# The last tiles of an entry: one product's weight sums made earlier, one operand's sums put behind the last tile

## The chip, the cores and the metric

The kernel runs on one core of a Trainium2 chip. Its time is the device time of one execution in microseconds (us); the median of three runs is 1895.14 us (1893.95 to 1895.23). A profiled execution gives the trace from which all rows below are taken. The engines are TensorE (PE, with its weight loads as PEld), VectorE (DVE), ScalarE (ACT), GpSimd (POOL) and the queue of SyncE (SP), which issues most DMAs. Each works through its own instructions in order, and they wait for each other by semaphores.

## The reference

A decoder block on 1024 tokens of width 1024, in float32:

```python
h = h + 0.5 * swiglu(rms_norm(h, ffn1_norm), w1, w3, w2)          # D_FF = 2816
u = rms_norm(h, mix_norm);  proj = u @ w_in                       # q, k, v, p, gates
y_attn = dilated_mixture_attention(q, k, v) @ w_branch_attn
y_pool = multiscale_pool(p, pool_w, pool_scale) @ w_branch_pool
h = h + (sigmoid(gA) * y_attn + sigmoid(gB) * y_pool) @ w_out
h = h + 0.5 * swiglu(rms_norm(h, ffn2_norm), w1, w3, w2)
return rms_norm(h, final_norm)
```

Three stages concern us: the two up-projections of the FFNs (`x @ w1`, `x @ w3`) and the mixer's input projection (`u @ w_in`). Each begins with the normalised rows of h, which have to be transposed before TensorE can contract over features.

## The kernel before

**Seven products.** The large matrix products are cut into 2 x 2 blocks and computed with seven block products instead of eight (the Strassen-Winograd form). One half of the split is by tokens (512 and 512), the other by features. Of the left matrix x there are four blocks b11, b21 (tokens 0 to 511) and b12, b22 (tokens 512 to 1023) and four sums:

t1 = b12 - b11, t2 = b22 - t1, t3 = t2 - b11 = b22 - b12, t4 = t2 - b21.

In the code: `first_less` makes t1 (line 467), `second` t2 (471), `third` t3 (474, into the bank that held b12), `fourth` t4 (478). The products are numbered m = 1 to 7: m=1 uses b11, m=2 b21, m=6 t2, m=7 t3, m=5 t1, m=4 t4, m=3 b22. On the weights' side there are sums as well: s1 for m=5, s2 = s1 - a11 for m=6, s3 for m=7, s4 for m=3 (`Quad.summed`, lines 370 to 383); m=1, 2 and 4 take blocks of weights as they were loaded.

**High and low parts.** For accuracy each operand is split into a part rounded to the form `float32r` (high) and the rest (low), and each block product is three groups of four matmuls (line 332): high x high, weights' high x operand's low, weights' low x operand's high. ACT makes the high part by a copy (line 320 for weights, 411 and 433 for x), and DVE or POOL makes the low part by a subtraction (line 323 for weights; 416 and 436 for x). What is subtracted from a PSUM bank is always DVE's here.

**The entry.** At the head of each of the three stages stands an entry (`Entry.run`). The first 512 tokens are already transposed, and b11 and b21 are known. The second 512 tokens come in four tiles t = 4 to 7 of 128. Meanwhile PE has the products m=1 and m=2 of the first few column pairs to do, which need b11 and b21 only. Per tile, in this order: a product; four transposes for b22 (line 409) and four for b12 (line 485), into one PSUM bank each; the outputs of products; the four sums of x with their parts; a second product. The next tile's rows are scaled by the norm (line 282) in between. After the last tile come m=6, 7, 5, 4, 3, for which t2, t3, t1, t4 and b22 of all four tiles must be there. The entry is run for the first FFN (around 40 to 60 us of the span), for the mixer (around 657 to 678) and for the second FFN (around 1252 to 1276). The whole stretch is in an order written out by hand: each engine gets its instructions as the code names them.

Names in it: `operand(i)` splits the weights of the entry's i-th product (their low part on POOL), `product(i)` issues its matmuls, `out(i)` takes its bank to SBUF. `Rows` are transposes with their high part, `Parts` the high part (`higher`, ACT) and low part (`lower`, DVE unless POOL is named) of a sum. `more(0, 1)` makes s1 of the first product after the entry (DVE, line 370), `more(0, 2)` makes s2 (POOL, line 374), `more(0)` splits the weights of m=6 and `more(1)` those of m=7 (making s3 first, DVE, line 378). The low part of weights outside the entry goes to DVE for each third split and to POOL otherwise: m=6's low part is POOL's in the first FFN and the mixer and DVE's in the second FFN; m=5's is DVE's in the first FFN and POOL's in the other two.

PSUM has four banks under the tag "acc" (transposes, t2, products m=6, 7, 4) and four under "mm" (m=1, 2, 5, 3). Half tiles under the tag "s" (four of them) hold the sums of weights.

Of the kernel before, what the change touches and what calls it, by code (L numbers as in the profile page):

```python
# [137 lines left out]
def tile_block(  # L138
# [29 lines left out]
    ve, ac, gp, pe = nc.vector, nc.scalar, nc.gpsimd, nc.tensor  # L168

    def sbuf(name, side="left", bufs=1):  # L170
        return tc.tile_pool(name=name, bufs=bufs, side=side, reuse_waits="tile")
# [7 lines left out]
    def bank(tag, name):  # L179
        return psum.tile([P, HALF], F32, tag=tag, name=name)  # L180
# [18 lines left out]
    h = []  # L199
# [98 lines left out]
    LOWS, HIGHS = slice(0, HALF), slice(HALF, S)  # L298

    def sums_of_x(pool, name, order, **kw):  # L300
        return {
            s: tuple(pool.tile([P, 4, HALF], F32R, name=f"x{part}_{s}_{name}", **kw) for part in ("hi", "lo"))
            for s in order
        }
# [31 lines left out]
    class Quad:  # L336
# [49 lines left out]
        def run(self, m, back=True):  # L386
            if m not in self.w:
                self.operand(m)
            w, n = self.w.pop(m), self.n
            x = {1: "b11", 2: "b21", 3: "b22", 4: "t4", 5: "t1", 6: "t2", 7: "t3"}[m]  # L390
            key = {1: "x", 2: "x", 5: "v", 3: "v"}.get(m, m)
            first = key not in self.bank
            if first:
                self.bank[key] = bank("mm" if key in ("x", "v") else "acc", f"u_{self.sv.name}{n}{m}")
            self.sv.product(self.bank[key], w, x, start=first)
            if m == 3 and back:
                raws.back(2)
            return self.bank[key]
# [39 lines left out]
    class Entry:  # L438
# [18 lines left out]
        def run(self, high, after, first=0):  # L457


            X = self.sv.X  # L460

            def scaled_rows(t):
                return high(t, 1)

            def first_less(p12, t):
                t1 = h[t][:, LOWS]
                ve.tensor_tensor(t1, p12, self.low[t - 4][:, LOWS], op=OP.subtract)
                return t1

            def second(s, t1, t2):  # L470
                ve.tensor_tensor(t2, s.flat, t1, op=OP.subtract)

            def third(t2, p, t):
                ve.tensor_tensor(p, t2, self.low[t - 4][:, LOWS], op=OP.subtract)

            def fourth(t2, t):
                t4 = h[t][:, HIGHS]
                ve.tensor_tensor(t4, t2, self.low[t - 4][:, HIGHS], op=OP.subtract)
                return t4

            def turned(y, t):
                p12 = bank("acc", f"x_b12_{t}")
                for j in range(4):
                    c = slice(j * P, (j + 1) * P)
                    pe.transpose(p12[:, c], y[:, c], ident)
                return p12

            def turned_rows(y, t, tag="acc"):
                return Rows(X, "b22", y[:, HIGHS], t, tag)

            y = scaled_rows(4)
            self.operand(first + 2)
            r4 = None
            for t in range(4, NT - 1):
                i = first + 2 * (t - 4)
                k = i + 1
                self.product(i)
                high(t + 1, 0)
                s = turned_rows(y, t)
                p12 = turned(y, t)  # L500
                self.out(i)
                if r4 is not None:
                    r4.higher()
                    r4.lower(gp)
                t1 = first_less(p12, t)
                t2 = bank("acc", f"x_t2_{t}")
                s.lower()
                second(s, t1, t2)
                self.product(k)
                y = scaled_rows(t + 1)  # L510
                r2 = Parts(X, "t2", t2, t)
                r1 = Parts(X, "t1", t1, t)
                third(t2, p12, t)
                r1.lower(gp)
                self.operand(k + 2)
                r2.lower()
                self.out(k)
                r3 = Parts(X, "t3", p12, t)
                r3.lower()
                r4 = Parts(X, "t4", fourth(t2, t), t, False)  # L520
                after(t)
                self.operand(i + 4)
                if t > 4:
                    self.more(0, 1)

            t = NT - 1
            i, k = i + 2, k + 2
            self.product(i)
            p12 = turned(y, t)
            s = turned_rows(y, t, "mm")  # L530
            r4.higher()
            r4.lower(gp)
            t1 = first_less(p12, t)
            t2 = bank("acc", f"x_t2_{t}")
            second(s, t1, t2)
            self.more(0, 2)
            r2 = Parts(X, "t2", t2, t)
            third(t2, p12, t)
            self.more(0)
            self.out(i)  # L540
            r2.lower()
            r3 = Parts(X, "t3", p12, t)
            r3.lower()
            self.product(k)
            r1 = Parts(X, "t1", t1, t)
            r4 = Parts(X, "t4", fourth(t2, t), t, False)
            self.more(1)
            r1.lower()
            r4.higher()
            self.out(k)  # L550
            s.lower()
            r4.lower()
            after(t)


# [364 lines left out]
    X = sums_of_x(scope.enter_context(sbuf("x1")), "f1", SUMS)  # L920
# [1100 lines left out]
    with tc.manual_schedule():  # L2021
# [8 lines left out]
        for q in range(N // 2):  # L2030
# [20 lines left out]
            u, i = divmod(q, NT // 2)  # L2051
# [450 lines left out]
```

## Time and profile before

| what | value |
|---|---|
| median of three runs | 1895.14 us |
| profiled execution | 1895.29 us |
| its span | 1893.5 us |
| PE busy | 1875.3 us (99%) |
| DVE busy | 1346.6 us (71%) |
| ACT busy | 774.1 us (41%) |
| POOL busy | 726.2 us (38%) |
| mean granted clock of TensorE | 0.997 |

The span is the time from the first to the last recorded instruction. In an order-of-time row the columns are start, duration, engine, line, operation, output <- inputs, shapes and how many instructions were merged; in brackets the engine's idle time before it and what released it. In a row of windows stand the window, its length, busy time with the number of instructions of PE, PEld, DVE, ACT and POOL, the granted clock of TensorE, the DMA engines' busy share and GB/s. Names of tiles: `x_b` and `x_t` are banks with transposed rows and with t2, `xhi_t`, `xlo_t`, `xhi_b`, `xlo_b` the parts of the sums and blocks of x, `wc` the parts of weights, `s_` the sums of weights, `raw` weights as loaded, `u_` the products' banks.

### The profile page before, as it was taken

The page shows a single profiled execution, that of the slowest core. Times are in us where ns is not written, and L with a number is a line of the kernel's source. Part 1 is how long each engine was busy: PE and PEld are TensorE (multiplying, and loading weights), DVE is VectorE, ACT ScalarE, POOL GpSimd, SP SyncE. Part 2 cuts the span into 40 slices and gives each one's busy share as a digit, 9 for nine tenths or more (in the row PEclk, how much of TensorE's full clock was granted, in tenths as well). Part 3 has the DMA queues.
Part 4 walks back from the last instruction along what each step waited for, and adds up shares of the span by engine and source line. Part 5 has one row for each costly group of instructions (what it writes and reads, how often), then busy time and mean ns, then how long its engine had stood idle before and what let it go on. Part 6 is the DMA issues. An engine that isn't in the chain of part 4 may idle for free. (4 is left out here: it accounts for less than half of the span.)

```text
span 1893.5 us, 24607 instructions
## 1 busy us (share of the span) xinstructions
PE 1875.3 (99%) x8758; PEld 1556.0 (82%) x8758; DVE 1346.6 (71%) x1982; ACT 774.1 (41%) x1395; POOL 726.2 (38%) x542
## 2 busy tenths in 40 slices
PE   9999999999999999999999999999999999999998
PEld 8788888888888878888888888878888888888886
DVE  6777666557786776557885897888665566577867
ACT  7423333333345543334445772363333323334344
POOL 5533333332223354444555357553333333312221
PEclk9999999999999999999999999999999999999999
DMA  6154423436565526675568878734432223354654
GB/s 247 44 196 160 139 91 110 134 117 211 177 230 195 183 84 206 227 231 198 215 237 313 318 228 292 268 148 143 143 127 105 83 102 117 138 193 158 227 195 145
DMA packets 146035, 334.98 MB, mean 177 GB/s; under 512 B 17784, under 2 KB 39288, under 8 KB 144376
## 3 DMA queue, kind: packets, MB, share of 16 engines
q1 hardware_dynamic: 142168, 322.55, 49.4%
q10 hardware_dynamic: 3744, 10.85, 1.6%
q8 instruction: 69, 1.13, 0.3%
q14 instruction: 54, 0.44, 0.1%
HBM read 232.76 MB, written 100.60 MB: 176 GB/s over the span
## 5 line engine op out<-in xcount | busy, mean ns | idle before, releaser
L860 PE MATMUL d_f<-bhi_f,ahi_f 128*128 128x512 f32 x616 | 240.2, 390 | 0.0
L860 PE MATMUL d_f<-bhi_f,alo_f 128*128 128x512 f32 x616 | 239.7, 389 | 0.0
L860 PE MATMUL d_f<-blo_f,ahi_f 128*128 128x512 f32 x616 | 239.6, 389 | 0.0
L817 POOL TENSOR_TENSOR alo_f<-g_f,ahi_f 128x512 fp32r<-128x512 f32 x60 | 87.8, 1480 | 271.7 <-ACT ahi_f L813 271.7
L332 PE MATMUL u_mixm<-xhi_t_mix,wc_mixm 128*128 128x512 f32 x608 | 158.2, 392 | 3.1 <-ACT wc_mixm L320 3.1
L332 PEld LDWEIGHTS u_mixm<-xhi_t_mix,wc_mixm 128*128 128x128 f32 x608 | 114.0, 189 | 27.1 <-ACT wc_mixm L320 3.8
L860 PEld LDWEIGHTS d_f<-bhi_f,ahi_f 128*128 128x128 f32 x616 | 115.6, 188 | 24.4 <-ACT h L420 0.5
L860 PEld LDWEIGHTS d_f<-bhi_f,alo_f 128*128 128x128 f32 x616 | 115.6, 188 | 24.0
L860 PEld LDWEIGHTS d_f<-blo_f,ahi_f 128*128 128x128 f32 x616 | 115.7, 188 | 23.8
L332 PE MATMUL u_mixm<-xhi_b_mix,wc_mixm 128*128 128x512 f32 x456 | 120.3, 391 | 0.0
L323 POOL TENSOR_TENSOR wc_mixm<-s_mixm,wc_mixm 128x512 fp32r<-128x512 f32 x52 | 76.8, 1479 | 104.6 <-ACT wc_mixm L320 98.1
L332 PEld LDWEIGHTS u_mixm<-xhi_b_mix,wc_mixm 128*128 128x128 f32 x456 | 84.9, 188 | 17.3
L320 ACT ACTIVATE wc_mixm<-s_mixm 128x512 fp32r<-128x512 f32 x76 | 47.0, 628 | 113.2 <-DVE s_mixm L374 54.7
L813 ACT ACTIVATE ahi_f<-g_f 128x1024 fp32r<-128x1024 f32 x84 | 81.9, 975 | 5.7 <-DMA g_f<-gs_f 5.7
L332 PE MATMUL u_mixm<-xlo_t_mix,wc_mixm 128*128 128x512 f32 x304 | 81.9, 391 | 0.0
L323 POOL TENSOR_TENSOR wc_mixm<-raw,wc_mixm 128x512 fp32r<-128x512 f32 x40 | 60.1, 1505 | 38.9 <-ACT wc_mixm L320 31.3
L2182 PE MATMUL wo<-w_o,o_hi 128*128 128x512 f32 x224 | 69.3, 390 | 0.0
L813 ACT ACTIVATE bhi_f<-s_f2w 128x512 fp32r<-128x512 f32 x55 | 32.9, 628 | 86.1 <-DVE s_f2w L835 67.1
L332 PEld LDWEIGHTS u_mixm<-xlo_t_mix,wc_mixm 128*128 128x128 f32 x304 | 57.6, 190 | 12.2
L813 ACT ACTIVATE bhi_f<-s_f1w 128x512 fp32r<-128x512 f32 x55 | 33.1, 629 | 83.5 <-DVE s_f1w L835 70.3
L817 DVE TENSOR_TENSOR alo_f<-g_f,ahi_f 128x1024 fp32r<-128x1024 f32 (+1 forms) x48 | 58.7, 1222 | 10.0 <-ACT ahi_f L813 10.0
L332 PE MATMUL u_mixm<-xlo_b_mix,wc_mixm 128*128 128x512 f32 x228 | 61.0, 389 | 0.0
(1350 smaller groups left out, 4764.5 us busy)
## 6 DMA issues: line engine op xcount, KB each, us to landing
g_f<-gs_f SPq DMA_DIRECT2D x70, 512.0 KB
gs_f<-y_f SPq DMA_DIRECT2D x88, 256.0 KB
raw<-in_w2a_dram SPq DMA_DIRECT2D x35, 512.0 KB
raw<-in_w2b_dram SPq DMA_DIRECT2D x35, 512.0 KB
gs_f<-gb_f SPq DMA_DIRECT2D x46, 256.0 KB
raw<-in_w1a_dram SPq DMA_DIRECT2D x22, 512.0 KB
raw<-in_w3a_dram SPq DMA_DIRECT2D x22, 512.0 KB
raw<-in_w1b_dram SPq DMA_DIRECT2D x22, 512.0 KB
```

The source lines that it names most:

```text
L320: ac.activation(w[:, 0], src, AF.Copy)
L323: eng.tensor_tensor(w[:, 1], src, w[:, 0].bitcast(F32), op=OP.subtract)
L332: pe.matmul(p, a, b, start=(start and n == 0), stop=(n == 11), skip_group_check=not start)
L813: ac.activation(hi[:, c], src, AF.Copy)
L817: eng.tensor_tensor(lo[:, d], src[:, o], hi[:, d].bitcast(F32), op=OP.subtract)
L860: pe.matmul(self.banks[m][t], l, r, start=(first and q == 0), stop=(last and q == 2))
L2182: pe.matmul(banks[m][t], l, r, start=(st == 0 and j == 0 and q == 0), stop=(st == 1 and j == 1 and q == 2))
```

## The change

1. s1 is made in tile 6, behind t2's low part, instead of at the end of tile 5; s2 right behind tile 6's stage instead of in the midst of tile 7.
2. In the last tile b22's transposes come ahead of b12's, the output of the first product of the tile comes up, and the weights of m=6 are split (`more(0)`) ahead of `third`.
3. The fourth sums and their parts: tile 4's parts are made in tile 5, behind t2, the low part on DVE instead of POOL. Tile 5's sum is still made in tile 5, but into a half tile of its own; its parts are put off behind the last tile. Tiles 6 and 7 have sum and parts behind the last tile, 6's bank with t2 being kept until then. Low parts: tile 5 on POOL, 6 and 7 on DVE.
4. The last tile's t1 has its low part on POOL instead of DVE.

```diff
             def fourth(t2, t):
-                t4 = h[t][:, HIGHS]
+                t4 = self.sv.half_tile("s", f"t4_{t}") if t == 5 else h[t][:, HIGHS]
                 ve.tensor_tensor(t4, t2, self.low[t - 4][:, HIGHS], op=OP.subtract)
                 return t4
...
-            r4 = None
+            r4 = {}
+
+            def take_fourth(t2, t):
+                r4[t] = Parts(X, "t4", fourth(t2, t), t, False)
+
             for t in range(4, NT - 1):
...
                 self.out(i)
-                if r4 is not None:
-                    r4.higher()
-                    r4.lower(gp)
                 t1 = first_less(p12, t)
...
                 second(s, t1, t2)
+                if t == 5:
+                    r4[4].higher()
+                    r4[4].lower()
                 self.product(k)
...
                 r2.lower()
+                if t == 6:
+                    self.more(0, 1)
                 self.out(k)
                 r3 = Parts(X, "t3", p12, t)
                 r3.lower()
-                r4 = Parts(X, "t4", fourth(t2, t), t, False)
+                if t < 6:
+                    take_fourth(t2, t)
                 after(t)
                 self.operand(i + 4)
-                if t > 4:
-                    self.more(0, 1)
+            self.more(0, 2)
 
             t = NT - 1
             i, k = i + 2, k + 2
             self.product(i)
+            s = turned_rows(y, t, "mm")
             p12 = turned(y, t)
-            s = turned_rows(y, t, "mm")
-            r4.higher()
-            r4.lower(gp)
+            self.out(i)
             t1 = first_less(p12, t)
-            t2 = bank("acc", f"x_t2_{t}")
+            before, t2 = t2, bank("acc", f"x_t2_{t}")
             second(s, t1, t2)
-            self.more(0, 2)
             r2 = Parts(X, "t2", t2, t)
+            self.more(0)
             third(t2, p12, t)
-            self.more(0)
-            self.out(i)
             r2.lower()
             r3 = Parts(X, "t3", p12, t)
             r3.lower()
             self.product(k)
+            self.more(1)
             r1 = Parts(X, "t1", t1, t)
-            r4 = Parts(X, "t4", fourth(t2, t), t, False)
-            self.more(1)
-            r1.lower()
-            r4.higher()
+            r1.lower(gp)
+            take_fourth(before, t - 1)
             self.out(k)
+            take_fourth(t2, t)
+            for n in (5, 6, 7):
+                r4[n].higher()
+                r4[n].lower(gp if n == 5 else ve)
             s.lower()
-            r4.lower()
             after(t)
```

## The prediction

> **What bounds the kernel now.** I read the page first (share of each engine), then TensorE's waits, then two-microsecond windows around the three waits found, then the order of time in them.
>
> ```profile
> PE 1875.3 (99%) x8758; PEld 1556.0 (82%) x8758; DVE 1346.6 (71%) x1982; ACT 774.1 (41%) x1395; POOL 726.2 (38%) x542
> ...
> PE u_mixm L332 <- ACT wc_mixm L320: 3.1, 2, 2.6
> PE u_f20a L332 <- ACT wc_f20a L320: 2.7, 2, 2.3
> PE u_f10a L332 <- ACT wc_f10a L320: 2.5, 1, 2.5
> ```
>
> PE is busy for 1875.3 of 1893.5 us, so whatever PE does not wait for is saved one for one. Three of its waits are long, one behind each entry: the first seventh-part product after it (m=6, multiplied with t2) waits for its weights' high part.
>
> ```profile
> 62.00:64.00 2.00, 2.00 (x7) 1.58 (x6) 1.63 (x3) 0.86 (x2) 0.73 (x1) 0.64 0.00 0
> 64.00:66.00 2.00, 2.00 (x6) 1.54 (x5) 2.00 (x5) 1.71 (x4) 1.00 (x1) 0.51 0.00 0
> ...
> 680.00:682.00 2.00, 1.25 (x3) 1.06 (x4) 0.44 (x2) 1.93 (x4) 1.26 (x2) 0.59 0.26 92
> 682.00:684.00 2.00, 2.00 (x6) 1.58 (x6) 2.00 (x4) 0.51 (x2) 0.06 (x1) 0.56 0.07 25
> ...
> 1278.00:1280.00 2.00, 1.68 (x6) 1.12 (x7) 1.84 (x4) 1.62 (x4) 0.00 (x0) 1.00 0.00 0
> ```
>
> Behind the first two waits the granted clock (third number from the end) falls to 0.51 to 0.64 for about 3.5 us; behind the third it stays 1.00. The order of time in the first entry says what the wait consists of:
>
> ```profile
> 50.21 0.67 DVE L370 TENSOR_TENSOR s_f10a<-raw 128x512 f32<-128x512 f32 x1
> 52.52 1.29 POOL L436 TENSOR_TENSOR xlo_t_f<-x,xhi_t_f 128x512 fp32r<-128x512 f32 x1
> 52.66 2.22 DVE L282 SCALAR_TENSOR_TENSOR x<-x,nst,gain_ffn 128x1024 f32<-128x1024 f32 x1
> 55.56 0.60 PE L409 MATMUL x_b<-ident,x 128*128 128x128 f32 x4
> 56.77 0.68 DVE L478 TENSOR_TENSOR x<-x_t,x 128x512 f32<-128x512 f32 x1
> 57.37 0.68 DVE L467 TENSOR_TENSOR x<-x_b,x 128x512 f32<-128x512 f32 x1
> 58.15 0.70 DVE L471 TENSOR_TENSOR x_t<-x_b,x 128x512 f32<-128x512 f32 x1
> 58.20 1.28 POOL L436 TENSOR_TENSOR xlo_t_f<-x,xhi_t_f 128x512 fp32r<-128x512 f32 x1 [0.91 <-ACT xhi_t_f L433]
> 58.89 0.60 ACT L433 ACTIVATE xhi_t_f<-x_t 128x512 fp32r<-128x512 f32 x1 [0.77 <-DVE x_t L471]
> 59.43 1.27 POOL L374 TENSOR_TENSOR s_f10a<-s_f10a,raw 128x512 f32<-128x512 f32 x1
> 59.52 0.70 DVE L474 TENSOR_TENSOR x_b<-x_t,x 128x512 f32<-128x512 f32 x1 [0.66 <-ACT xhi_t_f L433]
> 60.74 0.63 ACT L320 ACTIVATE wc_f10a<-s_f10a 128x512 fp32r<-128x512 f32 x1 [1.25 <-POOL s_f10a L374]
> 61.42 1.20 PE L332 MATMUL u_f10a<-xhi_t_f,wc_f10a 128*128 128x512 f32 x4 [2.53 <-ACT wc_f10a L320]
> 74.04 1.07 PE L332 MATMUL u_f10a<-xhi_b_f,wc_f10a 128*128 128x512 f32 x4
> 75.85 1.07 PE L332 MATMUL u_f10a<-xhi_b_f,wc_f10a 128*128 128x512 f32 x4
> ```
>
> PE is done with the entry at 61.42 - 2.53 = 58.89. The sum for m=6 (POOL, L374) stands in POOL's queue behind tile 6's fourth low part (58.20), which hangs on tile 6's fourth sum (DVE, 56.77). So 59.43, 60.74, 61.42 follow.
>
> A group of four matmuls takes (75.85 - 74.04) / 2 = 0.905 us, a product 3 x 0.905 = 2.72. From the entry's end to the fifth product (b22, at 74.04) four products are 10.86; the row says 74.04 - 58.89 = 15.15. **Lost at this entry: 4.29.** The same for the other two:
>
> ```profile
> 672.74 1.27 DVE L282 SCALAR_TENSOR_TENSOR hn_mix<-h,nst,gain_mix 128x1024 f32<-128x1024 f32 x1
> 674.85 0.60 PE L409 MATMUL x_b<-ident,hn_mix 128*128 128x128 f32 x4
> 680.75 2.08 PE L332 MATMUL u_mixm<-xhi_t_mix,wc_mixm 128*128 128x512 f32 x4 [2.57 <-ACT wc_mixm L320]
> 685.92 1.46 POOL L323 TENSOR_TENSOR wc_mixm<-s_mixm,wc_mixm 128x512 fp32r<-128x512 f32 x1 [0.23 <-ACT wc_mixm L320]
> 693.14 1.07 PE L332 MATMUL u_mixm<-xhi_b_mix,wc_mixm 128*128 128x512 f32 x4
> ...
> 1272.53 0.60 PE L409 MATMUL x_b<-ident,hn_f 128*128 128x128 f32 x4
> 1278.16 0.69 DVE L323 TENSOR_TENSOR wc_f20a<-s_f20a,wc_f20a 128x512 fp32r<-128x512 f32 x1 [1.17 <-ACT wc_f20a L320]
> 1278.18 1.19 PE L332 MATMUL u_f20a<-xhi_t_f,wc_f20a 128*128 128x512 f32 x4 [2.29 <-ACT wc_f20a L320]
> 1282.10 3.00 POOL L323 TENSOR_TENSOR wc_f20a<-s_f20a,wc_f20a 128x512 fp32r<-128x512 f32 x2 [4.63 <-ACT wc_f20a L320]
> 1290.31 1.07 PE L332 MATMUL u_f20a<-xhi_b_f,wc_f20a 128*128 128x512 f32 x4
> ```
>
> Mixer: end 678.18, 693.14 - 678.18 - 10.86 = **4.10**. Second FFN: end 1275.89, 1290.31 - 1275.89 - 10.86 = **3.56**. Together **11.95 us** is all that the change can touch; 1.76 and 1.53 of it are the slow clock.
>
> **The change part by part.** *Tiles 4 to 6.* DVE's first sum (L370) leaves the end of tile 5 for tile 6, behind t2's low part. POOL loses the fourth low parts of tiles 4, 5 and 6; tile 4's goes to DVE (+0.60, the step from 56.77 to 57.37). I cost that at nothing: the scaling it delays ran 2.22 while POOL worked on SBUF (row 52.66) and 1.27 alone (672.74), so what tile 4's part takes, the freed POOL gives back. Uncovered it is 0.6 on a scaling that has to be ready for the next transposes. No DMA is issued elsewhere: SP's queue and the depths of the weight stream stay as they are. Tile 5's t4 takes one of four half tiles until its low part is made; the fifth request is the sum for m=3, wanted only four products (10.86) behind the start of m=6, so nothing.
>
> *Start of m=6.* POOL, now without the L436 of 52.52 and 58.20, is through with L374 before it is wanted: t1's low part of tile 6 can begin near 53.4 (the scaling ends there without its cover, and ACT's part with it), then 1.28 for it, 0.55 for DVE's L370, 1.28 for the weights' low part and 1.27: 57.8. What remains is the chain of the last tile's own t2. The transposes' order is swapped, so x12 comes second and is there at 55.56 + 0.60 = 56.16. Then L467 at 56.20, L471 0.78 later (57.37 to 58.15) at 56.98, t2's high part 0.74 later (58.15 to 58.89) at 57.72, the weights' high part one ACT step of 0.52 later, done 0.63 after that at 58.87, PE at 58.92 where it is free at 58.89. Wait: 0.03. The mixer (transposes done 675.45) gives 678.21 against 678.18, the second FFN (1273.13) 1275.89 against 1275.89. The three waits and both slow stretches go. This chain has no slack: each further step in it is paid in full.
>
> *m=6, second group* wants t2's low part 0.905 after the start. DVE has L474 (which begins when ACT has left t2's bank, row 59.52) and then the low part: 59.68 for 59.83 in the first FFN, 678.97 for 679.12 in the mixer. In the second FFN the low part of m=6's weights is DVE's (row 1278.16); the change puts it ahead of L474, where DVE stands until ACT ends (1275.84): 1275.87, L474 1276.47, low part until 1277.75, while PE wants it at 1276.80. **Wait 1.00.** Queued behind it are t3's parts and m=7's sum.
>
> *m=7* waits for t3's low part, then DVE's sum, then ACT: 61.72 for 61.64, 681.01 for 680.93, 1279.83 for 1279.61. **0.08, 0.08, 0.22.** Tile 6's t2 holds its PSUM bank until its fourth sum at about 61.6; m=7 needs a bank at 61.72, so nothing, but only by 0.1.
>
> *m=5* is where the put-off work lands. Between the weights of m=7 and those of m=5, ACT has t1's high part and three fourth high parts (0.52 each), in the mixer also the output of the last product: ready 64.23 for 64.44, **684.02 for 683.73 (0.29)**, 1282.35 for 1282.55. The low parts cost more, for POOL and DVE do not read SBUF together:
>
> ```profile
> 64.83 0.61 ACT L433 ACTIVATE xhi_t_f<-x 128x512 fp32r<-128x512 f32 x1
> 65.00 1.29 POOL L323 TENSOR_TENSOR wc_f10a<-s_f10a,wc_f10a 128x512 fp32r<-128x512 f32 x1 [2.27 <-ACT wc_f10a L320]
> 65.35 0.61 ACT L320 ACTIVATE wc_f10a<-s_f10a 128x512 fp32r<-128x512 f32 x1
> 65.98 0.86 DVE L436 TENSOR_TENSOR xlo_t_f<-x,xhi_t_f 128x512 fp32r<-128x512 f32 x1
> 66.56 1.42 POOL L323 TENSOR_TENSOR wc_f10a<-raw,wc_f10a 128x512 fp32r<-128x512 f32 x1 [0.27 <-ACT wc_f10a L320]
> 66.76 1.77 DVE L323 TENSOR_TENSOR wc_f10a<-s_f10a,wc_f10a 128x512 fp32r<-128x512 f32 x1
> ```
>
> Each starts when the other's ends: POOL until 66.29, DVE until 66.84 (0.55 later), POOL until 67.98, DVE until 68.53. The one that stands waiting gets the next turn. After the change POOL has in this order m=7's weights, t1, tile 5's t4 (1.28 each), then the next weights; DVE has the t4 of tiles 6 and 7. In the mixer: POOL until 682.31 and 683.59, DVE 684.16, POOL 685.44, DVE 686.00, POOL (m=5's weights, row 685.92) 687.28; PE wants them at 684.02 + 1.81 = 685.83. **Wait 1.52.** Second FFN, also POOL (the second of row 1282.10): 1281.13, 1282.41, 1282.98, 1284.26, 1284.83, 1286.11, wanted at 1284.36: **1.80.** First FFN, where they are DVE's (row 66.76) and also stand behind b22's low part and one more POOL turn: POOL 64.30, DVE 64.87, POOL 66.15, DVE 66.75, POOL 68.03, DVE 68.60, wanted 66.25: **2.40.** If the turns overlap instead, these three are 0 (POOL would be through by 685 in the mixer); if one more POOL turn comes first, each is 1.28 longer. I take the turns as worked out, since the four rows show just this alternation.
>
> *Sum.* Lost after: 0.03 + 0.08 + 2.40 = 2.51; 0.03 + 0.08 + 0.29 + 1.52 = 1.92; 1.00 + 0.22 + 1.80 = 3.02. Together 7.45 instead of 11.95: **4.5 us saved**. The profiled execution took 1895.29 (span 1893.5, 1.8 around it): 1890.8, span 1889.0. It lies 0.15 above the median of the runs, so **1890.7**.
>
> **A rule against the clock's part.** The two slow stretches begin just behind waits of 2.53 and 2.57; 2.29 had none. The Trainium skill (page "TensorE: Matmul & The Clock Gate", Part 1 and "Why this matters for your kernels") has the clock halved after an idle window of about 3.4 us and warns of gaps above some 3 us only. By it waits of 2.5 us should not have slowed anything, the rows disagree, and I go by the rows.
>
> **The rivals.**
> *A, no queue at m=5.* The put-off parts slip between, as they would if the turns overlapped. Lost: 0.11 + 0.40 + 1.22 = 1.73, so 10.2 saved: 1885.1 at the end, some 1888 if half of the queue stays. For it: DVE has only two SBUF turns in that stretch. Against it: rows 65.98 and 66.76.
> *B, the slow clock comes back.* The 2.40 at m=5 is hardly shorter than 2.53. One slow stretch costs 1.76: 1892.5; two (the mixer too) 1894.0. For it: the length of the wait. Against it: 2.29 without one.
> *C, the slow stretches don't come from the waits* and stay, 1.76 + 1.53. Then 4.5 - 3.3 = 1.2 saved: 1894.0. This is what the rule above comes to. Against it: each of the two begins within 2 us of the end of a wait.
> *D, slower.* One more POOL turn stands ahead of m=5's low part at every entry (1.28 each), so its waits are 2.8 to 3.7 and each of them slows the clock (1.7). Lost: 2.51 + 1.92 + 3.02 + 3 x (1.28 + 1.7) = 16.4, 4.4 more than before: 1899.6. It is slower from the point where the waits at m=5 are together longer by 4.5 than my sum. Against it: it needs the worst order three times.
> *E, the sum moved is not what m=6 waits for.* Then m=6 starts as late as now and only order changes: 1895. Against it: the rows from 56.77 to 61.42 hang together without a gap.
>
> **How the numbers follow.** About 0.2% (3.8 us) is what a measurement of this kernel can tell from no change, so below 1891.3 is faster. Forecast 0.47 (from 1889 to 1892.5 by itself; two thirds of it faster), A 0.23 (faster), B 0.17, C 0.04, E 0.03 (no change), D 0.06 (slower). Faster 0.31 + 0.23 = 0.54, no change 0.16 + 0.17 + 0.04 + 0.03 = 0.40, slower 0.06. The range takes in A's end and B: 1885.0 to 1894.5.
>
> **What would show it.** In the changed profile, right: the three L332 waits on ACT at m=6 under 0.3, granted clock 1.00 in the windows behind the first two, L374 ending before t2's high part; a wait of about 1 us at the second FFN's t2 low part; waits of 1.5 to 2.4 at m=5's third group, on POOL in the mixer and the second FFN and on DVE in the first. Wrong: no wait at m=5 (A), a granted clock near 0.6 behind it (B, D), or one at the old places without a wait (C). Distance from the entry's end to b22's product should be 13.4, 12.8 and 13.9 instead of 15.15, 14.96 and 14.42.

## The result, and the profile after

The changed kernel takes 1891.11 us (median of 17 runs, 1890.57 to 1892.06), the kernel before on the same chips 1895.19 (17 runs, 1893.77 to 1896.37). The ratio is 0.9979, 95% interval 0.9972 to 0.9987: faster by 4.1 us, 0.21%. The prediction said 1890.7.

| | before | after |
|---|---|---|
| profiled execution, span | 1895.29, 1893.5 | 1891.69, 1889.9 |
| PE busy | 1875.3 | 1874.5 |
| mean granted clock | 0.997 | 0.999 |
| entry's last group to b22's product: first FFN, mixer, second FFN | 16.22, 16.02, 15.49 | 14.33, 13.84, 14.94 |

The last row is the ruler of this section: from the start of the entry's last group of four matmuls to the start of the first group of b22's product (m=3), the fifth product behind the entry. Without a wait that is thirteen groups (this last one and four products of three) of 0.905 us, 11.77. The three entries together went from 47.73 to 43.11: 4.62 us gained.

TensorE's waits after, with total, number and longest:

```profile
PE u_f10a L332 <- DVE wc_f10a L323: 1.7, 1, 1.7
PE u_f20a L332 <- POOL wc_f20a L323: 1.2, 1, 1.2
...
PE u_mixm L332 <- POOL wc_mixm L323: 0.8, 1, 0.8
PE u_f20a L332 <- DVE xlo_t_f L436: 0.7, 1, 0.7
PE u_mixm L332 <- ACT wc_mixm L320: 0.6, 1, 0.6
```

The three waits of 2.3 to 2.6 for the high part (line 320) of m=6's weights are gone. New ones stand in their place: for the low part of weights (line 323) in all three entries, and for a low part of x (line 436) in the second FFN. (The 0.6 of the last row lies at 738, some 50 us behind the mixer's entry, and is no part of this.) The windows behind the old waits, and in the third and fourth row those with and behind the new wait of 1.7 us; the granted clock is third from the end:

```profile
62.00:64.00 2.00, 2.00 (x10) 1.51 (x9) 1.47 (x4) 2.00 (x5) 1.79 (x2) 1.00 0.00 0
64.00:66.00 2.00, 2.00 (x11) 1.65 (x10) 2.00 (x2) 1.26 (x3) 2.00 (x2) 1.00 0.01 4
...
68.00:70.00 2.00, 1.26 (x5) 1.05 (x6) 2.00 (x4) 0.02 (x1) 0.14 (x1) 1.00 0.00 0
70.00:72.00 2.00, 2.00 (x10) 1.68 (x9) 1.90 (x3) 1.25 (x2) 1.30 (x1) 1.00 0.36 92
...
680.00:682.00 2.00, 2.00 (x10) 1.66 (x9) 0.39 (x2) 2.00 (x5) 2.00 (x2) 1.00 0.00 0
682.00:684.00 2.00, 1.93 (x9) 1.26 (x8) 2.00 (x2) 1.18 (x3) 2.00 (x3) 1.00 0.00 0
```

Both slow stretches are gone too, and the new wait brings none. The first entry in order of time:

```profile
55.90 0.60 PE L485 MATMUL x_b<-ident,x 128*128 128x128 f32 x4
...
56.54 0.69 DVE L467 TENSOR_TENSOR x<-x_b,x 128x512 f32<-128x512 f32 x1 [0.50 <-PE x_b L485]
56.54 1.29 POOL L374 TENSOR_TENSOR s_f10a<-s_f10a,raw 128x512 f32<-128x512 f32 x1
...
57.33 0.70 DVE L471 TENSOR_TENSOR x_t<-x_b,x 128x512 f32<-128x512 f32 x1
...
58.06 0.60 ACT L433 ACTIVATE xhi_t_f<-x_t 128x512 fp32r<-128x512 f32 x1 [0.88 <-DVE x_t L471]
58.17 1.07 PE L332 MATMUL u_f12b<-xhi_b_f,wc_f12b 128*128 128x512 f32 x4
58.56 0.62 ACT L320 ACTIVATE wc_f10a<-s_f10a 128x512 fp32r<-128x512 f32 x1
...
59.23 1.19 PE L332 MATMUL u_f10a<-xhi_t_f,wc_f10a 128*128 128x512 f32 x4
...
63.47 1.30 POOL L436 TENSOR_TENSOR xlo_t_f<-x,xhi_t_f 128x512 fp32r<-128x512 f32 x1
63.73 3.28 DVE L436 TENSOR_TENSOR xlo_t_f<-x,xhi_t_f 128x512 fp32r<-128x512 f32 x2 [0.53 <-ACT xhi_t_f L433]
...
64.73 1.74 POOL L436 TENSOR_TENSOR xlo_t_f<-s_f1t,xhi_t_f 128x512 fp32r<-128x512 f32 x1
...
65.95 1.07 PE L332 MATMUL u_f10a<-xlo_t_f,wc_f10a 128*128 128x512 f32 x4
66.43 1.71 POOL L323 TENSOR_TENSOR wc_f10a<-raw,wc_f10a 128x512 fp32r<-128x512 f32 x1
...
67.54 1.15 DVE L323 TENSOR_TENSOR wc_f10a<-s_f10a,wc_f10a 128x512 fp32r<-128x512 f32 x1
...
68.74 2.11 PE L332 MATMUL u_f10a<-xhi_t_f,wc_f10a 128*128 128x512 f32 x8 [1.73 <-DVE wc_f10a L323]
...
72.50 1.07 PE L332 MATMUL u_f10a<-xhi_b_f,wc_f10a 128*128 128x512 f32 x4
```

The sum for m=6 (L374) is made while the last tile's sums are still under way, and m=6 follows the entry by 59.23 - 58.17 = 1.06 instead of 0.905. Then comes the queue: DVE needs 3.28 us for two low parts (1.29 in an experiment below, where POOL does not hold it up), POOL 1.74 and 1.71 for operations like that of 63.47 (1.30), and m=5's low part (67.54) is there only at 68.7, 1.73 after PE was through with the group before.

### The profile page after: what moved, and what is told of

Same layout as the page of the kernel before. It is cut to its first block, busy times and chain, and to the rows that moved or that the text cites. A ratio compares the mean times of both kernels' runs of the same rounds, so it can differ in the third digit from the quotient of the medians.

```text
span 1889.9 us, 24612 instructions
## 1 busy us (share of the span) xinstructions
PE 1874.5 (99%) x8758; PEld 1554.0 (82%) x8758; DVE 1349.5 (71%) x1985; ACT 773.4 (41%) x1395; POOL 722.3 (38%) x539
## 4 chain that ended last, share of the span: by engine, by line
PE 53%; DVE 3%; ACT 2%; issue 1%; DMA 1%; POOL 1%; ACTq 0%; SPq 0%; DVEq 0%; POOLq 0%
PE u_mixm L332 15%; PE d_f L865 8%; PE wo L2187 4%; PE yp L1929 1%; PE u_f20b L332 1%; PE u_f21a L332 1%; PE u_f210b L332 1%; PE u_f210a L332 1%; PE u_f29b L332 1%; PE u_f29a L332 1%; PE u_f28b L332 1%; PE u_f28a L332 1%; PE u_f27b L332 1%; PE u_f27a L332 1%; PE u_f26b L332 1%
```

## The experiments

Shown for each: the edit against the changed kernel (in the first against the kernel before), what was expected, the time, and the three distances.

| kernel | median us | against before (95%) | first FFN | mixer | second FFN |
|---|---|---|---|---|---|
| before | 1895.19 | | 16.22 | 16.02 | 15.49 |
| changed | 1891.11 | 0.9972 to 0.9987 | 14.33 | 13.84 | 14.94 |
| sums only | 1889.18 | 0.9958 to 0.9981 | 14.06 | 13.66 | 13.70 |
| put off only | 1891.36 | 0.9972 to 0.9990 | 14.33 | 14.12 | 15.33 |
| m=5 first | 1889.27 | 0.9958 to 0.9981 | 12.52 | 14.03 | 14.45 |
| low part first | 1890.36 | 0.9965 to 0.9984 | 14.31 | 13.83 | 14.20 |
| t4 in its bank | 1887.50 | 0.9948 to 0.9975 | 12.36 | 12.93 | 14.51 |
| last three together | 1885.39 | 0.9939 to 0.9964 | 12.32 | 12.42 | 12.68 |

(The last two beside runs of the kernel before with a median of 1894.76.)

**Which half of the change brings the gain.** First the sums alone, in the kernel before:

```diff
                 r2.lower()
+                if t == 6:
+                    self.more(0, 1)
                 self.out(k)
...
                 self.operand(i + 4)
-                if t > 4:
-                    self.more(0, 1)
+            self.more(0, 2)
...
             second(s, t1, t2)
-            self.more(0, 2)
```

> The kernel before with one part of the change alone: the two sums for m=6 move as in the change (s1 behind t2's low part of tile 6, s2 behind tile 6), while the fourth sums and the last tile's order stay as they were. Distance from the last group of the entry to b22's product: 16.22, 16.02 and 15.49 us before, 14.33, 13.84 and 14.94 after the change, 11.77 without any wait. If the sums' place is what the gain comes from: m=6 starts some 1 us late in place of 2.5 (the fourth sum of tile 6 still stands ahead of the last tile's t1 on DVE), no slow clock, and no queue at m=5, since only t4's low part of tile 7 is left for it: distances near 13.3, time 1887 to 1889, below the changed kernel. Rival (the putting off is what frees m=6): m=6 starts about 2 us late and the time stays within 2 us of before.

Measured: 1889.18, 0.2 above the expected range and below the changed kernel. Its waits:

```profile
PE u_mixm L332 <- ACT wc_mixm L320: 2.0, 3, 0.7
PE u_f10a L332 <- ACT wc_f10a L320: 1.6, 2, 1.1
...
PE u_f20a L332 <- ACT wc_f20a L320: 0.8, 2, 0.4
```

The first FFN in order of time:

```profile
57.44 1.29 POOL L374 TENSOR_TENSOR s_f10a<-s_f10a,raw 128x512 f32<-128x512 f32 x1
...
58.69 1.27 POOL L436 TENSOR_TENSOR xlo_t_f<-x,xhi_t_f 128x512 fp32r<-128x512 f32 x1
...
60.12 1.21 PE L332 MATMUL u_f10a<-xhi_t_f,wc_f10a 128*128 128x512 f32 x4 [1.10 <-ACT wc_f10a L320]
```

The sum for m=6 (L374) now runs ahead of tile 6's fourth low part (L436), and m=6 waits 1.10, 0.68 and 0.38 us instead of 2.53, 2.57 and 2.29; what it still waits for is the chain of the last tile's own t2. Beside these there are waits of 0.51, 0.60 and 0.41 for m=7's high part, which the expectation did not have, and one of 0.2 for a low part of x in the second FFN. (The mixer's third wait lies at 738, outside the entry.) Nobody waits for a low part of weights, since of t4 only tile 7 is left for later. The distances are 13.7 to 14.1 where about 13.3 was expected. Moving two sums is worth 6.0 us by itself.

Then everything but these two sums (the putting off, the last tile's order and t1's low part on POOL):

```diff
-                if t == 6:
-                    self.more(0, 1)
...
                 self.operand(i + 4)
-            self.more(0, 2)
+                if t > 4:
+                    self.more(0, 1)
...
             second(s, t1, t2)
+            self.more(0, 2)
```

> The changed kernel with the two sums for m=6 back at their old places in the code (s1 at the end of tile 5, s2 behind t2 of tile 7). POOL's own order is the same as in the changed kernel, because the fourth low part that stood ahead of s2 is gone; only DVE's s1 stands earlier. By my reading the time is that of the changed kernel within 1 us (1890 to 1892), distances 14.3, 13.8, 14.9 within 0.4. Rival (moving the sums is a part of its own): m=6 late again by over 1 us per entry, time 1893 to 1895.

Measured: 1891.36, the changed kernel's time within 0.3 us. This half too clears POOL's way to L374, since the L436 that stood there is gone: m=6 waits for ACT at most 0.33 us. So each half removes most of the same wait; the second to be added has little left to remove, and the putting off brings a queue of its own. On top of this half, the sums' new place takes another 0.7 us from the distances (43.78 to 43.11), too little to show in the times. On top of the sums, the rest of the change costs 1.9 us (1889.18 to 1891.11). No run separates the putting off from the last tile's order and from t1's low part on POOL.

**What the new waits at m=5 are.** m=5's weights are split ahead of the put-off parts:

```diff
         def operand(self, m, eng=None):
+            if m in self.w:
+                return
             self.summed(m)
...
-                     lambda n, part=0: first.A.summed(6, part > 1, gp) if part else first.A.operand((6, 7)[n]))
+                     lambda n, part=0: first.A.summed(6, part > 1, gp) if part else first.A.operand((6, 7, 5)[n]))
...
             take_fourth(t2, t)
+            self.more(2)
             for n in (5, 6, 7):
```

> The changed kernel with the weights of m=5 split ahead of the put-off parts of t4 (on ACT, and on POOL or DVE) instead of behind them. If the waits left at m=5 (1.73, 0.81 and 1.23 us on their low part) come from the queue of put-off parts, all three go, and with them the restart of PE: distances some 12.4, 12.9 and 13.6, about 4 us less, 1886.5 to 1888. Rival (the put-off parts cost the same wherever they stand): the waits move to m=4, whose t4 low parts then come 1.3 us later, and the time stays at 1890 to 1892.

Measured: 1889.27. The three waits at m=5 are gone and the first FFN is nearly free of waits (12.52), but in the other two entries neither expectation came: a new wait stands at m=3. The mixer's rows:

```profile
680.26 3.54 DVE L438 TENSOR_TENSOR xlo_t_mix<-h,xhi_t_mix 128x512 fp32r<-128x512 f32 x2 [2.13 <-ACT xhi_t_mix L435]
...
686.91 0.69 DVE L1261 TENSOR_TENSOR y_m<-u_mixm,y_m 128x512 f32<-128x512 f32 x1
...
687.75 1.16 PE L332 MATMUL u_mixm<-xhi_b_mix,wc_mixm 128*128 128x512 f32 x4 [1.50 <-DVE y_m L1261]
```

m=3 is added into the bank of m=5 and waits until DVE has taken m=5's output from it (L1261); DVE is late because it stood 3.54 us at t4's two low parts; from there to L1261 it works almost without a pause.

The t4 of tiles 6 and 7 stays in PSUM:

```diff
-                t4 = self.sv.half_tile("s", f"t4_{t}") if t == 5 else h[t][:, HIGHS]
+                t4 = self.sv.half_tile("s", f"t4_{t}") if t == 5 else h[t][:, HIGHS] if t == 4 else t2
```

> The changed kernel with the fourth sums of tiles 6 and 7 left in the PSUM bank of their t2 instead of h's tile in SBUF. The order of all queues is the same; only DVE's two put-off low parts now read one operand from PSUM. If the wait at m=5 comes from DVE and POOL taking turns on SBUF: DVE does not wait for POOL there any more nor POOL for DVE, m=5's low part is ready about 66.6 for 66.9 in the first FFN (no wait), and some 0.2 and 0.5 us late in the mixer and the second FFN: distances 12.5, 13.1 and 14.2, time 1887.5 to 1889. Rival (the length of the queues is enough, whoever reads what): waits of 1.7, 0.8 and 1.2 stay, distances 14.3, 13.8, 14.9, time 1891.

Measured: 1887.50, 12.36, 12.93 and 14.51 for expected 12.5, 13.1 and 14.2. The same instructions in the same order, in the first FFN:

```profile
63.10 1.31 POOL L436 TENSOR_TENSOR xlo_t_f<-x,xhi_t_f 128x512 fp32r<-128x512 f32 x1
63.33 1.29 DVE L436 TENSOR_TENSOR xlo_t_f<-x_t,xhi_t_f 128x512 fp32r<-128x512 f32 x2 [0.48 <-ACT xhi_t_f L433]
64.36 1.29 POOL L436 TENSOR_TENSOR xlo_t_f<-s_f1t,xhi_t_f 128x512 fp32r<-128x512 f32 x1
...
65.13 1.07 DVE L323 TENSOR_TENSOR wc_f10a<-s_f10a,wc_f10a 128x512 fp32r<-128x512 f32 x1
65.61 1.76 POOL L323 TENSOR_TENSOR wc_f10a<-raw,wc_f10a 128x512 fp32r<-128x512 f32 x1
```

DVE's two low parts take 1.29 instead of 3.28, POOL's 1.31 and 1.29 although they run at the same time. With one operand in PSUM DVE and POOL do not stop each other; with both in SBUF they do (65.13 and 65.61 still show it). In the first FFN and the mixer the wait at m=5 is gone with the order of the queues unchanged, so there its cause is the turns on SBUF. In the second FFN 0.80 of 1.23 stays, where about 0.5 was expected:

```profile
1277.01 1.73 POOL L323 TENSOR_TENSOR wc_f20a<-s_f20a,wc_f20a 128x512 fp32r<-128x512 f32 x1
...
1278.79 2.11 PE L332 MATMUL u_f20a<-xhi_t_f,wc_f20a 128*128 128x512 f32 x8 [0.80 <-POOL wc_f20a L323]
```

There m=5's low part is POOL's, stands behind three other POOL operations, and takes 1.73 because the two engines still take turns at the weights. So the place in the queue counts too: with m=5's weights first there was no wait at m=5 in any entry.

**The second FFN's t2.** The split of m=6's weights goes behind t2's low part:

```diff
             r2 = Parts(X, "t2", t2, t)
-            self.more(0)
             third(t2, p12, t)
             r2.lower()
+            self.more(0)
```

> The changed kernel with the split of m=6's weights behind t2's low part of the last tile instead of ahead of t3's sum. DVE has that low part itself in the second FFN only: the wait of 0.73 us there for t2's low part goes (0.7 to 0.9 with the restart), if m=5's queue does not take it back; the other two entries keep their distances of 14.3 and 13.8. Time 1890 to 1891. Rival (it is taken back at m=5, since DVE and POOL are no earlier there): the wait at m=5 of the second FFN grows from 1.23 to about 2, time unchanged at 1891.

Measured: 1890.36, second FFN 14.20 instead of 14.94, the other two as they were. The wait of 0.73 for t2's low part was the price of that one place in the order.

**The three together:**

> The changed kernel with three edits together: m=5's weights split ahead of the put-off parts, m=6's weights split behind t2's low part, and the fourth sums of tiles 6 and 7 left in their PSUM bank. With m=5's weights first alone, m=3 waited for DVE's output of m=5 (1.5 us in the mixer, 0.9 in the second FFN), because DVE stood 3.5 us at two low parts of t4 against POOL. If the turns on SBUF are the cause of both, neither m=5 nor m=3 waits here: distances 12.2 to 12.7 in all three, time 1884 to 1886. Rival (DVE has too much to do behind the entry in any order): m=3 still waits about 1 us in two of them, time 1887 to 1889.

Measured: 1885.39, ratio 0.9952 (0.9939 to 0.9964), 9.4 us below the kernel before and the fastest kernel of this study. What TensorE still waits for in the weights of these stages:

```profile
PE u_mixm L332 <- ACT wc_mixm L320: 0.8, 1, 0.8
...
PE u_f20a L332 <- ACT wc_f20a L320: 0.3, 1, 0.3
```

The first wait lies at 735, some 50 us behind the mixer's entry; the second is m=7's. m=3 waits for nobody, and the mixer's two low parts of t4, from the order of time, take 1.29 instead of 3.54:

```profile
680.08 1.29 DVE L438 TENSOR_TENSOR xlo_t_mix<-x_t,xhi_t_mix 128x512 fp32r<-128x512 f32 x2 [2.08 <-ACT xhi_t_mix L435]
```

**How far the sum may be late, and what slows the clock.** The sum for m=6 is repeated on POOL, four times in all in one kernel, three times in the other:

```diff
-                eng.tensor_tensor(self.s2, self.s1, a11, op=OP.subtract)
+                for _ in range(4 if eng is gp and not self.sv.again else 1):
+                    eng.tensor_tensor(self.s2, self.s1, a11, op=OP.subtract)
+                self.sv.again = True
```

> The changed kernel with the sum s2 of the first product after each entry made four times on POOL instead of once (3 x 1.28 us of repeated work). If m=6 waits for that sum as soon as it is late: waits of about 3.1, 2.8 and 3.1 us at m=6. If waits of some 2.5 us and more are what slows the clock, a granted clock near 0.5 to 0.6 for about 3.5 us follows in all three entries, 1.5 to 1.8 us each; the put-off parts have time meanwhile and m=5 waits for nothing. Time 1898 to 1902. Rival (the slow stretches had another cause): the clock stays at 1.00 behind all three.

> The same with the sum made three times: waits of about 1.9, 1.5 and 1.8 us at m=6, shorter than any that was followed by a slow clock, so the granted clock stays at 1.00 behind all three. The waits at m=5 shrink by what m=6 waits. Time 1891 to 1893.5. Rival: a slow stretch here too, which would say that the length of the wait is not what decides.

Measured: fourfold 1900.08 (one run), waits of 3.4, 3.1 and 3.4, a slow clock in all three. Threefold 1895.64 (one run), above the expected range: waits of 2.06, 1.74 and 2.01, and against the expectation a slow clock behind the first and the third. The threefold kernel's waits in order of time:

```profile
60.97 0.73 PE L333 MATMUL u_f10a<-xhi_t_f,wc_f10a 128*128 128x512 f32 x2 [2.06 <-ACT wc_f10a L321]
...
679.83 1.19 PE L333 MATMUL u_mixm<-xhi_t_mix,wc_mixm 128*128 128x512 f32 x4 [1.74 <-ACT wc_mixm L321]
...
1277.04 1.18 PE L333 MATMUL u_f20a<-xhi_t_f,wc_f20a 128*128 128x512 f32 x3 [2.01 <-ACT wc_f20a L321]
```

Half-microsecond windows in which slow stretches begin, of the fourfold kernel (five rows, the second and the last with a stretch's end), of the threefold one and of the kernel before (two rows each):

```profile
62.00:62.50 0.50, 0.23 (x1) 0.23 (x2) 0.00 (x0) 0.50 (x2) 0.20 (x1) 0.79 0.00 0
65.50:66.00 0.50, 0.50 (x3) 0.45 (x2) 0.41 (x1) 0.50 (x2) 0.50 (x1) 0.79 0.00 0
683.50:684.00 0.50, 0.50 (x3) 0.36 (x2) 0.50 (x2) 0.00 (x0) 0.33 (x1) 0.52 0.00 0
1280.50:1281.00 0.50, 0.00 (x0) 0.00 (x0) 0.00 (x0) 0.18 (x1) 0.29 (x1) 0.85 0.00 0
1287.50:1288.00 0.50, 0.50 (x3) 0.43 (x2) 0.50 (x1) 0.50 (x2) 0.50 (x1) 0.82 0.00 0
```

```profile
62.00:62.50 0.50, 0.50 (x4) 0.41 (x3) 0.50 (x2) 0.00 (x0) 0.28 (x1) 0.97 0.05 16
1277.50:1278.00 0.50, 0.50 (x3) 0.39 (x2) 0.50 (x2) 0.00 (x0) 0.00 (x0) 0.61 0.00 0
```

```profile
62.50:63.00 0.50, 0.50 (x3) 0.40 (x2) 0.50 (x2) 0.36 (x1) 0.23 (x1) 0.55 0.00 0
680.00:680.50 0.50, 0.00 (x0) 0.00 (x0) 0.14 (x1) 0.43 (x1) 0.04 (x1) 0.86 0.22 82
```

Within the stretches the clock is 0.50 throughout, so a mean of 0.79 in 0.5 us puts the change of clock 0.21 before the window's end: 62.29, 683.52 and 1280.85 begin a stretch in the fourfold kernel, 65.71 and 1287.68 end one. The first stretch lasts 3.42, the third 6.83, twice that; the beginnings lie 621.23 and 1218.56 apart, 182.0 and 357.0 times 3.413. So the clock changes only on a grid of 3.413 us that takes no notice of the kernel's waits. The reading that fits is that what decides is how long PE stood still within one interval of it. In the threefold kernel the grid runs through 62.47 and 1277.61; the waits reach from 58.91 to 60.97, from 678.09 to 679.83 and from 1275.03 to 1277.04. Inside the interval that ends at the grid point they fill 1.91 (slow), 1.74 (not slow) and 2.01 (slow). In the kernel before, whose stretches begin at 62.55 and 680.36, it is 2.29 (slow), 2.18 (slow) and, for the second FFN's wait of 2.29, only 1.80, since the grid point 1277.69 cuts it (not slow). All six agree with a bound between 1.80 and 1.91 of 3.413 us. So do the fourfold kernel, whose waits fill 3.37, 2.40 and 2.73 of an interval (all slow), and the changed kernel, whose longest wait at the entries is 1.73 (not slow). Why the fourfold kernel's third stretch lasts two intervals is open; PE stood still for the first 0.65 us of it.

Where the grid lies in an execution is then chance. The times of the kernel before fit that: of its 31 runs beside the experiments the three with a mean granted clock of 1.000 took 1893.37 to 1893.84, those with 0.996 or 0.997 took 1894.67 to 1896.22. These runs have no trace that would show where their clock fell.

The Trainium skill ("TensorE: Matmul & The Clock Gate", Part 1) states a free-running window of 3413 ns, and the measured grid of 3.413 agrees. It also states that an idle window brings the half clock and, in "Why this matters for your kernels", warns of gaps above some 3 us only; here gaps of 2.01 and 2.06 already halved the clock, and the measurement decides.

## Why the prediction was right, and where not

**The waits at m=6 and the slow clock** were read rightly: POOL's L374 behind tile 6's fourth low part was the cause. The first experiment shows it, which moves that sum ahead and leaves the rest as it was; the second, which takes the low part away instead, agrees. Predicted was m=6 without a wait in all three, measured is 1.06 for 0.905 from group to group. L374 ends at 57.83, as forecast (57.8). The part put at nothing (tiles 4 to 6) held too: the scaling (L282) takes 1.28 in place of 2.22 in the first FFN, and TensorE's list of waits from 40 to 58 us is empty.

**The distances** by the prediction's own count (from the end of the entry's last group) were to be 13.4, 12.8 and 13.9; they are 13.26, 12.77 and 13.87. The entries gained 4.62 for 4.5. That the profiled execution gained 3.6 and the medians 4.1 is the rest of the kernel: already at the first entry's last group the changed profile runs 0.35 later (58.17 for 57.82). In three experiments with the changed kernel's order up to there that point lies at 57.80, 57.98 and 58.27, so a single profile doesn't tell such a difference from chance.

**The terms behind the sum were less good; by luck two errors nearly cancelled.** The first is a cost that the prediction did not have. PE has to start again after each short stop: the group behind a stop takes 0.13 to 0.16 us longer to the next one (starts at 59.23 and 60.26: 1.03 for 0.905). m=7 was to be late by 0.08, 0.08 and 0.22; measured from group to group it is 0.23, 0.23 and 0.34. The second is the step "**m=5 is where the put-off work lands**": waits of 2.40, 1.52 and 1.80 were forecast, and 1.73, 0.81 and 1.23 came. The turns were as forecast, POOL and DVE alternating, but in the first FFN the chain from the end of t1's low part to the end of m=5's took 3.92 instead of 4.30 (64.77 to 68.69): while DVE had a turn in between, each of POOL's ends came 1.70 and 1.67 after the last, not 1.85 and 1.88. And PE wanted the part at 66.86 instead of 66.25; of these 0.61, 0.35 is the profile's later start and the rest the restarts. With the restart behind them the losses at m=5 are 2.0, 1.15 and 1.5. The mixer's 0.29 for m=5's high part came out as 0.36 from group to group.

**The second FFN's t2 low part**: forecast 1.00, 0.73 of waiting and 1.02 from group to group (1274.36 - 1272.44 less 0.905).

**The rivals.** A (no queue) is refuted by the waits, though the bank experiment shows that its condition can nearly be made: 1887.5. B did not come, the clock stays at 1.00 behind m=5. Here luck had a part: a wait of 2.40, as forecast for the first FFN, would have been over the bound found above unless a grid point cut it, and the 1.73 that came is under it. C falls, since the slow stretches went with the waits; the threefold and fourfold kernels bring them back. D and E did not come.

**What the prediction did not see** is that it weighed the two halves as one. Its sum is made of a gain most of which either half brings, and of a queue that only one of them brings. It was also wrong in taking the length of a wait (2.29 or 2.53) for what slows the clock.

## What to carry to other kernels

When an operation that others wait for stands behind another in a queue, moving it ahead and removing what stands before it are alternatives, and only one needs paying for: cost each alone before adding them. Work that is put off lands in front of something else, so look for the next instruction behind it on every engine. Where VectorE and GpSimd both work from SBUF, leaving one operand in PSUM can be worth more than a new order of the queues: here 1887.50 against 1889.27 and 1890.36 for the two orders tried.

## What was not expected of the hardware

Two low parts on DVE took 3.28 us with both operands in SBUF beside a busy POOL and 1.29 with one in PSUM, and POOL's beside them 1.74 and 1.29. The clock changes on a grid of 3.413 us that runs on by itself: standing still for 1.91 of one interval halved it for the whole next one (once for two), and 1.80 did not, so a wait of 2.29 across a grid point cost no clock where one of 2.01 inside an interval did.
